# A recurrence's diagonal by elementwise products and a block of ones, and background TensorE work pinned behind the dense products

## The chip, the cores and the metric

One core of one Trainium2 chip runs the kernel. The metric is device time in microseconds (us) of one execution. Before the change the median of three runs is 1806.2 us (1805.67 to 1806.68). The profile is of one execution that took 1806.44 us; its span, from the first to the last instruction, is 1804.7 us, so 1.74 us lie around the span.

## The reference

One decoder layer on 256 positions of 2048 channels. A combined input projection feeds three branches (a gated delta rule with convolutions, the HGRN2 recurrence, attention into 256 memory tokens); gates mix them, and an MLP of width 8192 follows. What the change touches is the HGRN2 branch's matrix of scores within a chunk:

```python
def hgrn2(q, f, i, lb):
    ...
    def step(state, inp):
        q_i, k_i, v_i, b_i = inp
        dec = jnp.exp(jnp.where(causal[:, :, None], b_i[..., :, None, :] - b_i[..., None, :, :], -jnp.inf))
        a_i = jnp.einsum('bhtd,bhjd,bhtjd->bhtj', q_i, k_i, dec)
        o = (q_i * jnp.exp(b_i)) @ state + a_i @ v_i
```

On the diagonal (t = j) the decay is 1, so the diagonal of `a_i` is the sum over the 128 channels d of q times k.

## The kernel before

**Dense products.** Nearly all work is products of activations with weights streamed from memory. Weights come as blocks of 256 rows by 512 columns (one DMA of 512 KB by SyncE), are split by ScalarE (`wh`, L174) and VectorE (`wl = w - wh`, L175) into two fp32r parts, and TensorE sums three products: high by high, high by low, low by high. `unit` (L206 to L208) does it with 512 columns moving for each product, 12 products for a block; `unit_joined` puts the two parts of the activations side by side (L225, 512 columns) and adds the third product over 256 columns (L227). A `unit_joined` has 128 products in six pieces and writes two PSUM tiles, whose sums are taken out by ScalarE and VectorE (L265, L266) when their half is done; the pool has two such tiles, so the next unit's first half waits for the first tile to be read.

**Background steps.** The branches' own small work is written as Python generators in the list `bg`: `gen_start` (statistics, masks, transposes of x), `gen_ab`, `gen_c` (attention), `gen_a` (delta rule, once for each of two head groups), `gen_b` (HGRN2, once for each head group), `gen_merge`. After each piece of a dense unit `tick` adds the present rate to a credit, and `pump` runs as many steps (up to the next `yield`) of the first generator as the credit has whole numbers. A unit gives 8 ticks (a branch's own product 4), whatever its kind. The rates: 1.0 at the start, R1 while the delta rule's projections run, R2 in the memory branch's gates, R3 in the HGRN2 projections (`BF`, `BQ`, `BI`, `BZ` for each head group), R4 in branch 0's products. Steps from `ahead_of_all` (convolutions, gates) go in front of the list.

**Order.** The order in which the program is traced is a priority, not an order: the framework's scheduler, when it lays out each engine's queue, may put an instruction whose inputs it takes as ready ahead of older ones, and puts one that it takes as not ready behind younger ones. Each queue is then fixed, and an engine waits at its next instruction until that one's inputs are there. `pin` (`keep_in_program_order`) sets one instruction behind everything traced before it on its engine.

**The lines that matter below.** L495 (`gcol`), L498 (`pc`) and L507 (`pl`): three small transposes in three consecutive steps of `gen_start`. L637: four transposes of the softmax in `gen_c`. L793 to L800: the decay matrix of `gen_a`, in which VectorE writes `dl` (L796) and TensorE multiplies it (L798) within the same step. L1060 to L1067: the diagonal in `gen_b`; for each head and each half of the sequence a full 128x128 product of k and q in fp32 (L1064, 8 for a head group, which the trace shows as 16 records), of which VectorE keeps the diagonal by multiplying with the identity (L1066). L1127 to L1133: the predicated copies after the products `pa` (L1120).

Of the kernel before, what the change touches and what calls it, by code (L numbers as in the profile page):

```python
# [10 lines left out]
F32 = mybir.dt.float32  # L11
F32R = mybir.dt.float32r
I32 = mybir.dt.int32
AF = mybir.ActivationFunctionType
ALU = mybir.AluOpType
AX = mybir.AxisListType

P = 128
# [15 lines left out]
KG = 2  # L34
BL = 16
WB = 4
R1, R2, R3, R4 = 1.1, 1.0, 1.0, 1.2


@with_exitstack  # L40
def tile_trunk(ctx: ExitStack, tc, a):
    nc = tc.nc
    V, A, T, G = nc.vector, nc.scalar, nc.tensor, nc.gpsimd

    cst = ctx.enter_context(tc.tile_pool(name="cst", bufs=1))
    wp = ctx.enter_context(tc.tile_pool(name="wp", bufs=4))
# [15 lines left out]
    def g4(name, shape=(P, 1024), dt=F32):  # L62
        return gp.tile(list(shape), dt, tag="g", name=nm(name))
# [11 lines left out]
    def bank(name):  # L75
        return pbp.tile([P, 512], F32, tag="bp", name=nm(name))

    def const(name, shape, dt=F32):
        return cst.tile(list(shape), dt, tag=name, name=name)
# [8 lines left out]
    mem_r = a["mem"][0].rearrange("(t p) n -> p t n", p=P)  # L88
    x_r = a["x"][0].rearrange("(t p) n -> p t n", p=P)

    pin = tc.keep_in_program_order

    def adma(out, in_):
        tc.keep_in_program_order(nc.scalar.dma_start(out, in_))

# [32 lines left out]

    def pump(n=1):
        while n > 0 and bg:  # L130
            try:
                next(bg[0])
                n -= 1
            except StopIteration:
                bg.pop(0)

    def drain():
        while bg:
# [264 lines left out]


    mgt, mlt, caus = const("mgt", [P, P]), const("mlt", [P, P]), const("caus", [P, P])
    mgtr = const("mgtr", [P, P], F32R)
    msk2 = const("msk2", [P, 2, P])
    dblk = const("dblk", [P, BL])
    mblk = const("mblk", [P, P])
# [2 lines left out]
    def gen_masks():  # L412
        G.affine_select(out=mgt, in_=ones, pattern=[[-1, P]], base=0, channel_multiplier=1,
                        compare_op=ALU.is_gt, fill=0.0)
        G.affine_select(out=mlt, in_=ones, pattern=[[1, P]], base=0, channel_multiplier=-1,
                        compare_op=ALU.is_gt, fill=0.0)
        pin(V.tensor_tensor(out=caus, in0=mlt, in1=ident, op=ALU.add))
        pin(V.tensor_copy(mgtr, mgt))
        pin(V.tensor_copy(msk2[:, 0, :], mlt))
        pin(V.tensor_scalar(out=msk2[:, 1, :], in0=caus, scalar1=-1.0, scalar2=None, op0=ALU.mult))  # L420
        pin(V.tensor_reduce(out=dblk, in_=ident.rearrange("p (k c) -> p c k", c=BL), axis=AX.X, op=ALU.add))
        yield
        prev = ident
        for s in (1, 2, 4, 8, 16, 32, 64):
            b = 2 * s
            if b < P:
                cur = mblk if b == BL else cst.tile([P, P], F32, tag=f"blk{b.bit_length() % 2}", name=f"blk{b}")
                v3 = cur.rearrange("p (n s) -> p n s", s=b)
                G.affine_select(out=v3, in_=ones.rearrange("p (n s) -> p n s", s=b),
                                pattern=[[-b, P // b], [0, b]], base=0, channel_multiplier=1,  # L430
                                compare_op=ALU.is_ge, fill=0.0)
                G.affine_select(out=v3, in_=v3, pattern=[[b, P // b], [0, b]], base=b - 1,
                                channel_multiplier=-1, compare_op=ALU.is_ge, fill=0.0)
            else:
                cur = ones
            d = cst.tile([P, P], F32, tag="mdiff", name=f"mdiff{s}")
            pin(V.tensor_tensor(out=d, in0=cur, in1=prev, op=ALU.subtract))
            pin(V.tensor_tensor(out=mT[s], in0=d, in1=mlt, op=ALU.mult))
            prev = cur
            yield  # L440

    def bc(t, n):
        return t.unsqueeze(1).to_broadcast([P, n, P])
# [25 lines left out]
    def gen_start():  # L469
        V.tensor_copy(rsm, rstd_of(sumsq_of(ssm, "ssm"), NT, D))  # L470
        xs = []

        def load_x():
            c = len(xs)
            t = g4("x", (P, NT, 512))
            pin(nc.sync.dma_start(t, x_r[:, :, c * 512:(c + 1) * 512]))
            xs.append(t)

        masks = gen_masks()
        grow = load_grow(["g_pre_mix", "g_pre_mlp"], 16, adma)  # L480
        crow = const("crow", [96, P])
        adma(crow, a["conv_a"][0].rearrange("t (c p) -> (t c) p", p=P))
        lrow = const("lrow", [8, P])
        adma(lrow, a["lb_raw"][0].rearrange("(c p) -> c p", p=P))
        load_x()
        yield
        pb = bank("rb")
        for t in range(NT):
            rr = g4("rr", (P, P))
            V.tensor_scalar(out=rr, in0=ones, scalar1=rsm[:, t:t + 1], scalar2=None, op0=ALU.mult)  # L490
            T.matmul(pb[:, t * P:(t + 1) * P], rr, ident, start=True, stop=True)
        V.tensor_copy(rbm, pb[:, 0:S])
        yield
        load_x()
        turn_grow(grow, 32, 16)  # L495
        yield
        pc = bank("pc")
        T.transpose(pc[:, 0:96], crow, ident[0:96, 0:96])  # L498
        V.tensor_copy(ccol, pc[:, 0:96])
        for nm_, t in (("gn_a", gna), ("gn_b", gnb)):  # L500
            adma(t, a[nm_][0:1, :].to_broadcast([P, P]))
        adma(alog, a["a_log"][0:1, :].to_broadcast([P, 8]))
        adma(dtb, a["dt_bias"][0:1, :].to_broadcast([P, 8]))
        yield
        load_x()
        pl = bank("pl")
        T.transpose(pl[:, 0:8], lrow, ident[0:8, 0:8])  # L507
        raw, e, lb = small("raw", 8), small("e", 8), small("lb", 8)
        V.tensor_copy(raw, pl[:, 0:8])
        V.tensor_tensor(out=e, in0=raw, in1=raw, op=ALU.subtract)  # L510
        exp_ln_table(e, e)
        pin(A.activation(e, e, AF.Exp))
        re = small("re", 8)
        V.reciprocal(re, e)
        pr = small("pr", 8)
        V.tensor_tensor(out=pr, in0=e, in1=re, op=ALU.mult)
        V.tensor_tensor(out=lb, in0=pr, in1=pr, op=ALU.subtract)
        pin(A.activation(lbl1, lb, AF.Ln, bias=1.0, scale=-1.0))
        c1, c2 = small("c1", 8), small("c2", 8)
        V.tensor_scalar(out=c1, in0=lb, scalar1=TINY, scalar2=None, op0=ALU.max)  # L520
        pin(A.activation(c1, c1, AF.Ln))
        V.tensor_scalar(out=c2, in0=lb, scalar1=0.0, scalar2=-1e30, op0=ALU.is_le, op1=ALU.mult)
        V.tensor_tensor(out=lba, in0=c1, in1=c2, op=ALU.add)
        yield
        st = small("ssx", 8)
        sumsq_chunk(xs[0], st, 0)
        yield
        load_x()
        A.activation(alog, alog, AF.Exp)
        next(masks)  # L530
        yield
        sumsq_chunk(xs[1], st, 1)
        yield
        next(masks)
        yield
        sumsq_chunk(xs[2], st, 2)
        yield
        next(masks)
        yield
        sumsq_chunk(xs[3], st, 3)  # L540
        yield
        next(masks)
        yield
        rx = rstd_of(sumsq_of(st, "ssx"), NT, D)

        def scale(c):
            for t in range(NT):
                V.tensor_scalar(out=xs[c][:, t, :], in0=xs[c][:, t, :], scalar1=rx[:, t:t + 1],
                                scalar2=None, op0=ALU.mult)

        scale(0)
        yield
        for c in range(4):
            if c < 3:
                scale(c + 1)
            hc = h8("hh")
            hB[c], hT[c] = hc, (hc[:, :, 0, :], hc[:, :, 1, :])
            transpose_chunk(xs[c], hT[c], c, 16)
            yield
        yield from masks  # L560
# [209 lines left out]
    def gen_a(hg, kc, qc, vc, z):  # L770
# [20 lines left out]
        dec = g4("dec", (P, 8, P))  # L791
        for t in range(NT):
            dl = g4("dl", (P, 2, 4, P), F32R)  # L793
            pd = bank("dec")
            for i, l_ in enumerate((ldh, ldl)):
                V.tensor_tensor(out=dl[:, i], in0=bc(caus, 4),  # L796
                                in1=l_.bitcast(F32)[:, t, hs].unsqueeze(2).to_broadcast([P, 4, P]), op=ALU.mult)
                T.matmul(pd, mgtr, dl[:, i].rearrange("p h i -> p (h i)"), start=i == 0, stop=i == 1)  # L798
            A.activation(dec[:, t * 4:t * 4 + 4, :], pd.rearrange("p (h i) -> p h i", h=4), AF.Exp)
            yield  # L800
# [239 lines left out]
    def gen_b(hg, k, g, q, v, z):  # L1040
# [17 lines left out]
        yield  # L1058

        AT = g4("AT", (P, 8, P))  # L1060
        for t in range(NT):
            pd = bank("ad")
            for h in range(4):
                T.matmul(pd[:, h * P:(h + 1) * P], k[:, h, t * P:(t + 1) * P], q[:, h, t * P:(t + 1) * P],  # L1064
                         start=True, stop=True)
            V.tensor_tensor(out=AT.rearrange("p (h t) i -> p h t i", t=NT)[:, :, t, :],  # L1066
                            in0=pd.rearrange("p (h i) -> p h i", h=4), in1=bc(ident, 4), op=ALU.mult)  # L1067
        yield
        kps = [g4("kp0", (P, 4, S)), g4("kp1", (P, 4, S))]
        qp = lp.tile([P, 8, BL * BL], F32, tag="lb", name=nm("qp"))  # L1070
# [352 lines left out]
```

## Time and profile before

| | before |
|---|---|
| median of 3 runs | 1806.2 us |
| profiled execution | 1806.44 us |
| its span | 1804.7 us |
| TensorE products busy | 1793.5 us, 99% |
| TensorE weight loads busy | 1532.6 us, 85% |
| VectorE busy | 1127.0 us, 62% |
| ScalarE busy | 905.6 us, 50% |
| TensorE's share of the chain that ended last | 97% |
| granted TensorE clock | 1.0 in every stage but the tail |

A busy TensorE is not yet one without losses: the end of a product's record is modelled and reaches over the start of the next, so a short wait leaves no idle time in the table. What a product costs is read from start to start of neighbouring products.

### The profile page before, as it was taken

What the parts mean: (1) busy time and instruction counts of PE and PEld (TensorE: products, weight loads), DVE (VectorE), ACT (ScalarE), POOL (GpSimd) and SP (SyncE); (2) the same over time, 40 slices, a digit from 0 to 9 for tenths busy, and PEclk for the clock granted to TensorE, in tenths of its full rate; (3) what the DMA queues carried; (4) which work ended last, traced back from release to release, by engine and by line L of the source; (5) the groups of instructions that cost most, each with busy time, mean ns of one, the idle gap of its engine ahead of it and who ended that gap; (6) DMA issues with size and microseconds to landing.
All of it is one profiled execution on the core that took longest, in us unless ns stands there. A gap on an engine that the chain in (4) does not pass through costs nothing.

```text
span 1804.7 us, 23851 instructions
## 1 busy us (share of the span) xinstructions
PE 1793.5 (99%) x9241; PEld 1532.6 (85%) x9241; DVE 1127.0 (62%) x1518; ACT 905.6 (50%) x1156; POOL 44.5 (2%) x68
## 2 busy tenths in 40 slices
PE   9999999999999999999999999999999999999998
PEld 7888888888888888888888888888888888888886
DVE  5865678755764677696555557655655565655556
ACT  6645565544555565555444445544444444444433
POOL 1000000200200000000000000000000000000000
PEclk9999999999999999999999999999999999999999
DMA  8665645754665556465666674666666676666664
GB/s 264 207 194 160 185 146 168 209 172 138 177 187 152 158 169 187 141 186 175 198 186 187 213 232 152 191 193 191 195 186 198 188 220 187 195 187 195 188 194 139
DMA packets 174946, 333.40 MB, mean 185 GB/s; under 512 B 13144, under 2 KB 14832, under 8 KB 174576
## 3 DMA queue, kind: packets, MB, share of 16 engines
q1 hardware_dynamic: 169280, 325.10, 58.7%
q10 hardware_dynamic: 4528, 4.54, 0.9%
q0 software_dynamic: 1024, 2.23, 0.7%
q8 instruction: 72, 1.18, 0.3%
q14 instruction: 42, 0.34, 0.1%
HBM read 329.60 MB, written 2.23 MB: 184 GB/s over the span
## 4 chain that ended last, share of the span: by engine, by line
PE 97%; DVE 1%; DMA 1%; ACT 1%; issue 0%; SPq 0%; DVEq 0%; POOLq 0%; POOL 0%; ACTq 0%
PE mm L225 23%; PE mm L206 18%; PE mm L207 18%; PE mm L208 18%; PE mm L227 12%; PE pa L1120 1%; DMA w<-in_w_kv_mem 0%; PE pzt L921 0%; PE pw L916 0%; PE mm L373 0%; PE mm L375 0%; PE mm L372 0%; DVE wl L175 0%; DMA w<-in_w_in 0%; DVE cv L718 0%
## 5 line engine op out<-in xcount | busy, mean ns | idle before, releaser
L175 DVE TENSOR_TENSOR wl<-w,wh 128x1024 fp32r<-128x1024 f32 x600 | 728.5, 1223 | 540.2 <-ACT wh L174 456.3
L174 ACT CAST wh<-w 128x1024 fp32r<-128x1024 f32 x600 | 628.0, 1052 | 719.0 <-PE mm L208 453.7
L206 PE MATMUL mm<-wh,hh 128*128 128x512 f32 x576 | 227.5, 395 | 0.3 <-DVE sum L266 0.3
L208 PE MATMUL mm<-wh,hh 128*128 128x512 f32 x576 | 224.7, 390 | 0.0
L225 PE MATMUL mm<-h2h,wh 128*128 128x512 f32 x960 | 224.4, 390 | 0.0
L207 PE MATMUL mm<-wl,hh 128*128 128x512 f32 x576 | 224.4, 390 | 0.0
L225 PEld LDWEIGHTS mm<-h2h,wh 128*128 128x128 f32 x960 | 178.3, 188 | 35.8
L206 PE MATMUL mm<-wh,mh 128*128 128x512 f32 x512 | 199.2, 389 | 0.0
L207 PE MATMUL mm<-wl,mh 128*128 128x512 f32 x512 | 199.2, 389 | 0.0
L208 PE MATMUL mm<-wh,ml 128*128 128x512 f32 x512 | 199.2, 389 | 0.0
L225 PE MATMUL mm<-hh,wh 128*128 128x512 f32 x768 | 184.8, 391 | 0.3 <-ACT z L730 0.3
L225 PEld LDWEIGHTS mm<-hh,wh 128*128 128x128 f32 x768 | 141.0, 188 | 27.8 <-ACT z L730 0.5
L208 PEld LDWEIGHTS mm<-wh,hh 128*128 128x128 f32 x576 | 108.1, 188 | 22.7
L206 PEld LDWEIGHTS mm<-wh,hh 128*128 128x128 f32 x576 | 108.2, 188 | 21.8 <-DVE sum L266 0.5
L207 PEld LDWEIGHTS mm<-wl,hh 128*128 128x128 f32 x576 | 108.3, 188 | 21.1
L227 PEld LDWEIGHTS mm<-h2h,wl 128*128 128x128 f32 x960 | 119.3, 192 | 2.3
L227 PE MATMUL mm<-h2h,wl 128*128 128x256 f32 x960 | 120.3, 283 | 0.0
L207 PEld LDWEIGHTS mm<-wl,mh 128*128 128x128 f32 x512 | 96.1, 188 | 20.0
L208 PEld LDWEIGHTS mm<-wh,ml 128*128 128x128 f32 x512 | 96.1, 188 | 19.9
L206 PEld LDWEIGHTS mm<-wh,mh 128*128 128x128 f32 x512 | 96.1, 188 | 19.9
L227 PE MATMUL mm<-hh,wl 128*128 128x256 f32 x768 | 102.2, 284 | 0.0
L227 PEld LDWEIGHTS mm<-hh,wl 128*128 128x128 f32 x768 | 98.9, 191 | 3.4
(388 smaller groups left out, 1913.9 us busy)
## 6 DMA issues: line engine op xcount, KB each, us to landing
w<-in_w_in SPq DMA_DIRECT2D x240, 512.0 KB, 4.0
w<-in_w_mlp_in SPq DMA_DIRECT2D x128, 512.0 KB, 4.0
w<-in_w_mlp_out SPq DMA_DIRECT2D x128, 512.0 KB, 4.2
w<-in_w_out SPq DMA_DIRECT2D x32, 512.0 KB, 4.1
w<-in_w_kv_mem SPq DMA_DIRECT2D x30, 512.0 KB, 4.9
w<-in_w_br_c SPq DMA_DIRECT2D x16, 512.0 KB, 4.1
w<-in_w_br_a SPq DMA_DIRECT2D x16, 512.0 KB, 4.5
w<-in_w_br_b SPq DMA_DIRECT2D x16, 512.0 KB, 3.6
```

What stands on the lines that cost most here:

```text
L174: q(A.copy(wh[:, js, 0:width], w[:, js, 0:width]))
L175: q(V.tensor_tensor(out=wl[:, js, 0:width], in0=w[:, js, 0:width], in1=wh.bitcast(F32)[:, js, 0:width], op=ALU.subtract))
L206: T.matmul(o, st, wh[:, j, :], start=kt == 0, stop=False)
L207: T.matmul(o, st, wl[:, j, :], start=False, stop=False)
L208: T.matmul(o, sl, wh[:, j, :], start=False, stop=kt == nk - 1)
L225: T.matmul(ps[c], wh[:, j, c * P:(c + 1) * P], both[j], start=k0 + j == 0, stop=end)
L227: T.matmul(ps[c][:, 0:S], wl[:, j, c * P:(c + 1) * P], both[j][:, 0:S], start=False, stop=end)
L1120: T.matmul(pas[h][:, t * 192:t * 192 + 192], kp[:, h, t * P:(t + 1) * P], qp[:, h * 2 + t, 0:192], start=True, stop=True)
```

## The change

`gen_b` no longer forms full products for the diagonal. VectorE multiplies k and q elementwise for a whole head group (`kq`), ScalarE and VectorE split that into two fp32r parts (`kqh`, `kql`), and TensorE multiplies a 128x128 block of ones with each, 512 columns at a time; every row of the result then holds the sums over the channels, and VectorE keeps the diagonal as before. It takes three steps where it took one. `gen_a` makes `dl` in one step and multiplies it in the next, twice. `gen_start` has one more `yield`, ahead of the `pl` transpose. The first TensorE instruction of every background step is pinned. Rates R2 to R4 rise.

```diff
-R1, R2, R3, R4 = 1.1, 1.0, 1.0, 1.2
+R1, R2, R3, R4 = 1.1, 1.05, 1.05, 1.27
...
-    V, A, T, G = nc.vector, nc.scalar, nc.tensor, nc.gpsimd
+    V, A, G = nc.vector, nc.scalar, nc.gpsimd
+
+    pin = tc.keep_in_program_order
+    step_begins = [False]
+
+    class T:
+
+
+        @staticmethod
+        def placed(ins):
+            if step_begins[0]:
+                pin(ins)
+                step_begins[0] = False
+            return ins
+
+        @staticmethod
+        def matmul(*args, **kwargs):
+            return T.placed(nc.tensor.matmul(*args, **kwargs))
+
+        @staticmethod
+        def transpose(*args, **kwargs):
+            return T.placed(nc.tensor.transpose(*args, **kwargs))
...
     def pump(n=1):
         while n > 0 and bg:
+            step_begins[0] = True
             try:
                 next(bg[0])
                 n -= 1
             except StopIteration:
                 bg.pop(0)
+            step_begins[0] = False
...
-    mgtr = const("mgtr", [P, P], F32R)
+    mgtr, onesr = const("mgtr", [P, P], F32R), const("onesr", [P, P], F32R)
...
+        pin(V.tensor_copy(onesr, ones))
...
         load_x()
+        yield
         pl = bank("pl")
...
             dl = g4("dl", (P, 2, 4, P), F32R)
-            pd = bank("dec")
             for i, l_ in enumerate((ldh, ldl)):
                 V.tensor_tensor(out=dl[:, i], in0=bc(caus, 4),
                                 in1=l_.bitcast(F32)[:, t, hs].unsqueeze(2).to_broadcast([P, 4, P]), op=ALU.mult)
+            yield
+            pd = bank("dec")
+            for i in range(2):
                 T.matmul(pd, mgtr, dl[:, i].rearrange("p h i -> p (h i)"), start=i == 0, stop=i == 1)
...
         AT = g4("AT", (P, 8, P))
-        for t in range(NT):
-            pd = bank("ad")
-            for h in range(4):
-                T.matmul(pd[:, h * P:(h + 1) * P], k[:, h, t * P:(t + 1) * P], q[:, h, t * P:(t + 1) * P],
-                         start=True, stop=True)
-            V.tensor_tensor(out=AT.rearrange("p (h t) i -> p h t i", t=NT)[:, :, t, :],
-                            in0=pd.rearrange("p (h i) -> p h i", h=4), in1=bc(ident, 4), op=ALU.mult)
+        kq, kqh, kql = g4("kq"), g4("kqdh", dt=F32R), g4("kqdl", dt=F32R)
+        V.tensor_tensor(out=kq, in0=k.rearrange("p h s -> p (h s)"), in1=q.rearrange("p h s -> p (h s)"), op=ALU.mult)
+        yield
+        A.copy(kqh, kq)
+        V.tensor_tensor(out=kql, in0=kq, in1=kqh.bitcast(F32), op=ALU.subtract)
+        yield
+        for hp in range(2):
+            pd, cs = bank("ad"), slice(hp * 512, hp * 512 + 512)
+            T.matmul(pd, onesr, kqh[:, cs], start=True, stop=False)
+            T.matmul(pd, onesr, kql[:, cs], start=False, stop=True)
+            V.tensor_tensor(out=AT[:, hp * 4:hp * 4 + 4, :], in0=pd.rearrange("p (b i) -> p b i", b=4), in1=bc(ident, 4),
+                            op=ALU.mult)
         yield
```

## Rows read from the trace of the kernel before

**Rows 1.** The page: busy us (share) and instructions; the chain's shares by engine.
```profile
PE 1793.5 (99%) x9241; PEld 1532.6 (85%) x9241; DVE 1127.0 (62%) x1518; ACT 905.6 (50%) x1156; POOL 44.5 (2%) x68
...
PE 97%; DVE 1%; DMA 1%; ACT 1%; issue 0%; SPq 0%; DVEq 0%; POOLq 0%; POOL 0%; ACTq 0%
```

**Rows 2.** Costliest groups: operation xcount | busy us, mean ns | idle before, releaser.
```profile
L175 DVE TENSOR_TENSOR wl<-w,wh 128x1024 fp32r<-128x1024 f32 x600 | 728.5, 1223 | 540.2 <-ACT wh L174 456.3
L174 ACT CAST wh<-w 128x1024 fp32r<-128x1024 f32 x600 | 628.0, 1052 | 719.0 <-PE mm L208 453.7
```

**Rows 3.** The chain in order of time: start us, us, what.
```profile
633.35 1.79 PE ad L1064 x16
769.65 1.78 PE ad L1064 x16
1133.24 7.28 PE mm L225 x32
```

**Rows 4.** Timeline, TensorE at both `dec`: start us, us, operation xcount [idle <-releaser].
```profile
275.27 0.63 PE L225 MATMUL mm<-hh,wh 128*128 128x512 f32 x2
...
276.41 0.19 PEld L798 LDWEIGHTS dec<-dl,mgtr 128*128 128x128 f32 x1 [0.24 <-DVE dl L796]
...
276.75 2.93 PE L225 MATMUL mm<-hh,wh 128*128 128x512 f32 x12
...
460.06 0.39 PE L208 MATMUL mm<-wh,ocl 128*128 128x512 f32 x1
...
461.29 0.40 PE L207 MATMUL mm<-wl,och 128*128 128x512 f32 x1
```

**Rows 5.** Timeline, TensorE around the transposes of `gen_start`.
```profile
36.33 0.48 PE L206 MATMUL mm<-wh,memT 128*128 128x512 f32 x1
...
36.74 0.24 PE L106 MATMUL gcol<-ident,grow 32*128 32x32 f32 x1
...
37.14 0.22 PE L507 MATMUL pl<-ident,lrow 8*128 8x8 f32 x1
...
37.63 0.40 PE L208 MATMUL mm<-wh,memT 128*128 128x512 f32 x1
```

**Rows 6.** Timeline, TensorE around two small transposes of another step.
```profile
159.40 0.88 PE L227 MATMUL mm<-hh,wl 128*128 128x256 f32 x6
160.21 0.30 PE L673 MATMUL abt<-ident,abT 32*128 32x32 f32 x2
160.44 0.96 PE L225 MATMUL mm<-hh,wh 128*128 128x512 f32 x3
```

**Rows 7.** Timeline, TensorE at the start of the second head group's `AK`.
```profile
257.07 0.60 PE L637 MATMUL pT<-ident,p 128*128 128x128 f32 x4
...
257.43 0.72 PE L227 MATMUL mm<-hh,wl 128*128 128x256 f32 x4
...
258.46 2.12 PE L225 MATMUL mm<-hh,wh 128*128 128x512 f32 x8 [0.32 <-ACT z L730]
```

**Rows 8.** Timeline where `BQ` of head group 1 gives way to `BI`.
```profile
664.48 1.11 PE L227 MATMUL mm<-hh,wl 128*128 128x256 f32 x8
...
665.13 0.67 DVE L266 TENSOR_TENSOR sum<-mm,sum 128x512 f32<-128x512 f32 x1
...
665.86 0.50 PE L206 MATMUL mm<-wh,hh 128*128 128x512 f32 x1 [0.26 <-DVE sum L266]
```

**Rows 9.** Timeline, VectorE and TensorE ahead of the second diagonal.
```profile
762.34 1.21 DVE L175 TENSOR_TENSOR wl<-w,wh 128x1024 fp32r<-128x1024 f32 x1
...
764.28 0.39 PE L207 MATMUL mm<-wl,hh 128*128 128x512 f32 x1
...
768.01 1.22 DVE L1056 TENSOR_TENSOR bm<-bm,bd 128x1024 f32<-128x1024 f32 x1
```

**Rows 10.** Who waited for whom, 190 to 660 us: us in total, times, longest.
```profile
PEld oc L604 <- ACT pT L281: 0.5, 2, 0.3
```

More of the change, by code (lines that the diff above doesn't have):

```diff
@@ L89, in tile_trunk @@
     x_r = a["x"][0].rearrange("(t p) n -> p t n", p=P)
-    pin = tc.keep_in_program_order
     def adma(out, in_):
```

## The prediction

> **What bounds the kernel now.** I read the shares and the chain first, then the chain in order of time, then the timeline wherever TensorE's products stand further apart than usual. TensorE is busy for 99% of the span and makes up 97% of the chain [rows 1]; VectorE's and ScalarE's largest groups are the weight splits, and before them both engines idle for hundreds of microseconds, ScalarE mostly until TensorE gives a weight buffer back [rows 2]. So the splits are ahead and TensorE sets the end. Its price for a product is read from start to start: 32 products over 512 columns take 7.28 us, 0.2275 each [rows 3]. The reader is to see that a TensorE instruction saved is time saved nearly one to one, that work on the other engines is free as long as the splits stay ahead, and that the waits left on TensorE are few and below a microsecond each [rows 4, 7, 8, 10].
>
> **The change part by part.** The sum is made against the profiled execution, 1806.44 us, which lies 0.24 above the median of the runs; the 0.24 comes off at the end.
>
> *The diagonal.* Removed: for each of two head groups 8 fp32 products, 16 records, 1.79 and 1.78 us of the chain [rows 3]. Added: for each group 4 fp32r products over 512 columns, whose form the dense ones have, 4 x 0.2275 = 0.91. Both lie on TensorE's path: 3.57 - 1.82 = 1.75 us saved. If the ones cost as much as the two `dec` products with their waits do, (1.48 - 3 x 0.2275) / 2 = 0.40 each (the 1.48 is worked out below) [rows 4], only 0.38 is left; I take 1.75, since with their inputs made a step earlier they stand as the dense products do. The Trainium skill (TensorE: Matmul & The Clock Gate, Back-to-back issue gap) gives about 131 ns as the sustained spacing of products over 512 columns; by that the new ones would cost 0.52 a group, the saving would be 2.53 and the time 0.78 lower. This trace has 0.2275, so the trace decides.
>
> Off the path the diagonal adds an elementwise product (1.22 us for this shape on VectorE [rows 9]), a cast (1.05 on ScalarE) and a subtraction (1.22 on VectorE) [rows 2], 3.49 us a group and 7.0 in all; the two multiplications with the identity stay. The cover is the lead of the splits. It is thinnest just ahead of the second diagonal: a split that ends at 763.55 is used at 764.28, 0.73 later [rows 9]. The new VectorE work comes behind it. It costs nothing while the lead there is over 1.22, and at most 2.44 - 0.73 = 1.7 if both VectorE operations come ahead of one split with such a lead. I take 0, because ScalarE and VectorE idle before most splits [rows 2]. The copy that makes the block of ones is a single operation in the early masks and costs nothing.
>
> *The decay matrix.* `dl` and its product are in one step now, and TensorE waits for VectorE [rows 4]. From 275.27 to 276.75 start five products (two dense, `dec`, dense, `dec`), 1.48 us instead of 5 x 0.2275 = 1.14; from 460.06 to 461.29 four, 1.23 instead of 0.91. The split into two steps puts a step's worth of dense products between, so I take back 0.34 + 0.32 = 0.66; the bounds are 0 and 0.66. Two steps more for each delta-rule group only shift what follows.
>
> *The pins.* I counted ticks and steps through the program and compared each background step's place with TensorE's order in the trace. Only four first instructions stand ahead of their place, so only there does a pin move anything. Three are `gcol`, `pc` and `pl`: they stand within 0.6 us, between an L206 and the L207 of the same triple [rows 5], where the program has 12 products between each two. Together with two dense products they take 37.63 - 36.33 = 1.30 us, so 0.85 without those. Apart, each visit pays for its own way in and out: two small transposes of another step begin 0.09 late (six products of 0.12 from 159.40 end at 160.12), take 0.23, and the dense ones behind them lose 0.11 (0.96 - 0.39 = 0.57 for two spacings) [rows 6]. With one transpose each that is some 0.36, three times 1.08: 0.23 lost. Bounds 0 and 3 x 0.43 - 0.85 = 0.44. The queues that these steps are moved past lose nothing that I see: SyncE's third load of x stays in its step, the fourth and what follows come one step, some 2.7 us, later, and the transposes of x they feed run two dense units before their first use.
>
> The fourth is the softmax's transposes (L637), which my count puts 12 products later. Now they fill 0.36 us (257.07 to 257.43) of a time in which TensorE must wait anyway for ScalarE to empty PSUM (`z`, which releases it at 258.46) [rows 7]. Behind the pin TensorE reaches that wait 0.36 earlier and does the transposes later: 0.36 lost. Bounds 0 (ScalarE comes to `z` earlier) and 0.44. Behind a pinned instruction younger dense products may still be put ahead of it, so no queue is blocked by a pin alone.
>
> *Shifted steps.* Where a joined unit ends, the next one waits for VectorE to empty a PSUM tile. At 664.48 eight products of 0.12 should end at 665.44, and the next starts at 665.86, 0.42 late, because the predicated copies of L1127 to L1133 were ahead of L266 on VectorE [rows 8]. With two more steps and R3 at 1.05 my count puts the `pa` products before those copies exactly at the end of that unit, so the copies fall behind L266, and this wait goes. But some seven such boundaries get other background work beside them, and one of seven was hit before. I take 0, with 0.42 either way. The step budget closes as before: by the count, the last TensorE step of HGRN2 falls behind the last product of branch 0 with either set of rates, so no steps pile up at the drain.
>
> Sum: -1.75 - 0.66 + 0.23 + 0.36 = -1.82; 1806.44 - 1.82 - 0.24 = 1804.4 us.
>
> **The rivals.** In all, 0.2% (3.6 us) is about what a measurement of this kernel can tell from no change.
>
> (a) The pins don't move what I say (the four are held back by something else, or the scheduler fills the places alike): without the 0.59 it is 1803.8. For: only four of some hundred steps are concerned.
>
> (b) A wash: the `dec` waits return one step later, one more boundary is hit (0.42), and one split comes late by 1: 1806.2 - 1.75 + 0.59 + 0.42 + 1 = 1806.5. For: leads as short as 0.73 [rows 9].
>
> (c) VectorE becomes the bound where HGRN2 runs. The place is the second head group's start, the price at most all of the new work, 7.0, less what TensorE saves (1.75 + 0.66): 1806.2 + 7.0 - 2.4 = 1810.8, slower by 0.25%. It decides from the point where the new work eats the lead of several splits in a row; against it speak the idle times before the splits [rows 2].
>
> (d) Everything aligns: the waits for `pT` (0.5 [rows 10]), for `z` (257.43 plus four products is 257.99, the next starts at 258.46: 0.47 [rows 7]) and the boundary's 0.42 go as well, and the pins cost nothing: 1806.2 - 1.75 - 0.66 - 0.5 - 0.47 - 0.42 = 1802.4, faster by 0.21%. Against: by my count the steps of the attention (`gen_c`), where the first two of these waits lie, keep their places, R1 being unchanged.
>
> (e) TensorE is not the bound: weight loads are busy for 85% [rows 1], and if the rest is room, the saved products fall into it and the time stays at 1806.2. The Trainium skill (Perfetto Trace Analysis, Identifying the Most-Contended Engine) says to judge TensorE by weight loads, not by product time. The chain and the even spacing of 0.2275 speak against that here [rows 1, 3].
>
> **How the numbers follow.** Forecast 1804.4: 0.62. (a) 1803.8: 0.10. (b) 1806.5: 0.12. (c) 1810.8: 0.06. (d) 1802.4: 0.07. (e) 1806.2: 0.03. The forecast's own bounds are 1806.2 - 1.75 - 0.66 - 0.42 = 1803.4 and, with `dec` giving nothing, the pins at 0.88 and a boundary at 0.42, 1805.8. To leave out no more than 2 in 10 the range takes in (a), (e) and the most of (b): 1802.9 to 1806.5. Faster by over 0.2%: 0.07, (d). Slower: 0.06, (c). Within: 0.87.
>
> **What would show it.** In the changed kernel's trace: the `ad` products 0.91 us a group and spaced as dense ones; `dec` without VectorE as releaser; `gcol`, `pc`, `pl` a dozen dense products apart; the L637 transposes of the fourth head behind the wait for `z`, and that wait near 0.8; no wait for `sum` at the end of the second `BQ`. It is wrong if TensorE shows idle time released by a weight split around the second diagonal, or if the time leaves the span's TensorE work by more than the waits listed.

## The result and the profile after

| | before | after |
|---|---|---|
| median of 5 runs | 1806.02 us (1805.67 to 1806.68) | 1813.54 us (1812.92 to 1815.8) |
| profiled execution | 1806.44 us | 1812.92 us |
| its span | 1804.7 us | 1811.2 us |

The ratio is 1.0044, with a 95% interval of [1.0034, 1.0055]: the change made the kernel 7.5 us slower. The forecast was 1804.4 us, its range ended at 1806.5, and of the rivals only (c) had a slower end, with 1810.8 and another place.

In the listing after, every TensorE product has L60 and every transpose L64 (the wrapper's lines); a weight split is `wl` L196 and `wh` L195, a joined unit's sum L286 and L287, the forward substitution L903 to L914.

The page's list of the costliest groups, in the columns of [rows 2], has one new entry: idle time ahead of TensorE's dense products that VectorE's `sum` ended.

```profile
PE 1794.2 (99%) x9217; PEld 1530.7 (85%) x9217; DVE 1130.5 (62%) x1523; ACT 907.6 (50%) x1158; POOL 40.1 (2%) x68
...
L60 PE MATMUL mm<-hh,wh 128*128 128x512 f32 x768 | 185.8, 393 | 5.5 <-DVE sum L287 4.7
```

The busy shares are those of [rows 1]; they hide the loss. The view of who waited for whom, TensorE alone over the whole span (us in total, times, longest), names it:

```profile
PE mm L60 <- DVE sum L287: 4.7, 1, 4.7
...
PE mm L60 <- ACT z L753: 0.8, 1, 0.8
...
PE mm L60 <- DVE wl L196: 0.2, 1, 0.2
```

One wait of 4.7 us stands out of a list in which nothing from the kernel's middle had reached 1. The timeline of TensorE there, where `BF` of the first head group gives way to `BQ`:

```profile
528.58 3.82 PE L60 MATMUL mm<-hh,wh 128*128 128x512 f32 x16
532.23 1.11 PE L60 MATMUL mm<-hh,wl 128*128 128x256 f32 x8
538.08 3.41 PE L60 MATMUL mm<-hh,wh 128*128 128x512 f32 x8 [4.74 <-DVE sum L287]
541.29 1.38 PE L60 MATMUL mm<-hh,wl 128*128 128x256 f32 x8
542.50 2.00 PE L60 MATMUL mm<-hh,wh 128*128 128x512 f32 x8
```

The eight products over 256 columns from 532.23 take some 0.95 (eight equal ones in e5 below, from 535.20 to 536.15), so TensorE was ready at 533.18 and began at 538.08, 4.90 late. And then it is slow: the first eight take 541.29 - 538.08 = 3.21 where 8 x 0.2275 = 1.82 [rows 3] would do. The table by windows (us, TensorE's busy time and instructions, granted clock, DMA share, GB/s) shows why:

```profile
533.00:538.00 5.00, 0.34 (x3) 1.00 0.42 131
538.00:541.50 3.50, 3.42 (x9) 0.57 0.49 151
541.50:545.00 3.50, 3.50 (x22) 0.94 0.00 0
```

After the idle time the granted clock is 0.57 for 3.5 us, near the lower of its two levels (1.2 of 2.4 GHz), then 0.94. The two lots of eight products after the wait lose 1.39 and 0.25. The place costs 4.90 + 1.64 = 6.5 of the 6.5 us by which the two spans differ.

VectorE at that place (start us, us, operation):

```profile
521.55 1.23 DVE L196 TENSOR_TENSOR wl<-w,wh 128x1024 fp32r<-128x1024 f32 x1 [2.91 <-ACT wh L195]
522.85 0.17 DVE L903 MEMSET lb<- 128x128 f32 x1
...
536.12 1.22 DVE L914 TENSOR_TENSOR X<-xc,mblk 128x1024 f32<-128x1024 f32 x1
537.26 1.28 DVE L287 TENSOR_TENSOR sum<-mm,sum 128x512 f32<-128x512 f32 x2
```

and in the kernel before:

```profile
517.48 0.17 DVE L878 MEMSET lb<- 128x128 f32 x1
...
529.72 1.23 DVE L889 TENSOR_TENSOR X<-xc,mblk 128x1024 f32<-128x1024 f32 x1
530.87 0.68 DVE L266 TENSOR_TENSOR sum<-mm,sum 128x512 f32<-128x512 f32 x1
```

with the TensorE products that this `sum` lets begin:

```profile
532.82 1.98 PE L225 MATMUL mm<-hh,wh 128*128 128x512 f32 x8
```

Between `lb` and `X` lies the second delta-rule group's forward substitution: fifteen pairs of small operations (a product and a reduction, 0.17 to 0.29 each), every one of which needs the one before, with some weight splits among them. In both kernels the whole block, 13.4 us before and 14.4 after from `lb` to the start of `sum`, stands ahead of `sum` in VectorE's queue. Before, `sum` ended at 531.55 and TensorE needed it at 532.82: 1.27 to spare. Now the chain begins behind one split more, 5.4 us later (522.85 - 517.48), and is 1.0 longer, for it has five splits inside where it had four. Less the 1.27 and the 0.36 by which TensorE itself comes later (533.18 against 532.82), that is 4.8 of the 4.9. ScalarE's part of the sum is there long before VectorE comes to it:

```profile
533.43 1.06 ACT L286 COPY sum<-mm 128x512 f32<-128x512 f32 x2
```

From 534.49 on, only `X` and what stands ahead of it hold `sum`. (ScalarE is late as well: two splits went ahead of L286. With VectorE free at 534.0, when the first half is there, `sum` would end at 534.7 and TensorE would still have waited 1.5.)

The other places, by the difference in start of the same dense product in the two traces (counted from the first): 0.62 is lost between products 96 and 192, 0.66 more by product 2360, 6.87 from there to product 2688 (the place above, and 0.3 besides), 1.38 is won back by product 3136, 0.37 by 3712, and 0.17 lost to the end.

The remaining rows of after that answer to those of before. The small transposes of `gen_start`, to be held against [rows 5]:

```profile
36.28 0.48 PE L60 MATMUL mm<-wh,memT 128*128 128x512 f32 x1
36.88 0.50 PE L60 MATMUL mm<-wl,memT 128*128 128x512 f32 x1
37.22 0.63 PE L60 MATMUL mm<-wh,memT 128*128 128x512 f32 x2
...
39.61 0.24 PE L64 MATMUL gcol<-ident,grow 32*128 32x32 f32 x1
...
42.67 0.25 PE L64 MATMUL pc<-ident,crow 96*128 96x96 f32 x1
...
48.34 0.22 PE L64 MATMUL pl<-ident,lrow 8*128 8x8 f32 x1
```

The softmax's transposes [rows 7], the second group's decay matrix [rows 4] and the second diagonal [rows 3], with the late split ahead of it [rows 9]:

```profile
259.13 2.12 PE L60 MATMUL mm<-hh,wh 128*128 128x512 f32 x8 [0.75 <-ACT z L753]
...
261.57 0.60 PE L64 MATMUL pT<-ident,p 128*128 128x128 f32 x4
...
463.95 0.39 PE L60 MATMUL mm<-wh,ocl 128*128 128x512 f32 x1
464.32 0.47 PE L60 MATMUL dec<-dl,mgtr 128*128 128x512 f32 x1
464.63 0.40 PE L60 MATMUL mm<-wh,och 128*128 128x512 f32 x1
464.86 0.48 PE L60 MATMUL dec<-dl,mgtr 128*128 128x512 f32 x1
465.18 0.40 PE L60 MATMUL mm<-wl,och 128*128 128x512 f32 x1
...
771.35 0.50 PE L60 MATMUL mm<-wl,hh 128*128 128x512 f32 x1 [0.19 <-DVE wl L196]
...
779.42 0.40 PE L60 MATMUL ad<-kqdh,onesr 128*128 128x512 f32 x1
...
780.36 0.39 PE L60 MATMUL mm<-wh,hh 128*128 128x512 f32 x1
```

The four new products of the diagonal take 780.36 - 779.42 = 0.94.

### The profile page after: what moved, and what is told of

Read it like the earlier page. It is cut to its first block, busy times and chain, and to the rows that moved or that the text cites. A ratio compares the mean times of both kernels' runs of the same rounds, so it can differ in the third digit from the quotient of the medians.

```text
span 1811.2 us, 23809 instructions
## 1 busy us (share of the span) xinstructions
PE 1794.2 (99%) x9217; PEld 1530.7 (85%) x9217; DVE 1130.5 (62%) x1523; ACT 907.6 (50%) x1158; POOL 40.1 (2%) x68
## 4 chain that ended last, share of the span: by engine, by line
PE 83%; DVE 2%; ACT 1%; issue 1%; POOL 0%; DVEq 0%; POOLq 0%
PE mm L60 78%; PE pa L60 1%; PE pzt L60 1%; PE pw L60 1%; DVE wl L196 0%; PE kk L60 0%; PE o L60 0%; PE bo L60 0%; PE tr L64 0%; PE y L60 0%; PE mgT L64 0%; PE X L64 0%; DVE xc L911 0%; DVE tm L910 0%; ACT wh L195 0%
## 5 line engine op out<-in xcount | busy, mean ns | idle before, releaser
L196 DVE TENSOR_TENSOR wl<-w,wh 128x1024 fp32r<-128x1024 f32 x600 | 729.0, 1223 | 540.8 <-ACT wh L195 460.8
L195 ACT CAST wh<-w 128x1024 fp32r<-128x1024 f32 x600 | 628.4, 1052 | 723.1 <-PE mm L60 642.6
L60 PE MATMUL mm<-wh,hh 128*128 128x512 f32 x1152 | 366.4, 392 | 0.0
L60 PEld LDWEIGHTS mm<-wh,hh 128*128 128x128 f32 x1152 | 216.1, 188 | 44.0
L60 PE MATMUL mm<-wl,hh 128*128 128x512 f32 x576 | 224.7, 390 | 0.2 <-DVE wl L196 0.2
L60 PE MATMUL mm<-h2h,wh 128*128 128x512 f32 x960 | 224.4, 390 | 0.0
L60 PEld LDWEIGHTS mm<-h2h,wh 128*128 128x128 f32 x960 | 178.3, 188 | 35.8
L60 PE MATMUL mm<-wh,mh 128*128 128x512 f32 x512 | 199.2, 389 | 0.0
L60 PE MATMUL mm<-wl,mh 128*128 128x512 f32 x512 | 199.2, 389 | 0.0
L60 PE MATMUL mm<-wh,ml 128*128 128x512 f32 x512 | 199.2, 389 | 0.0
L60 PE MATMUL mm<-hh,wh 128*128 128x512 f32 x768 | 185.8, 393 | 5.5 <-DVE sum L287 4.7
L60 PEld LDWEIGHTS mm<-hh,wh 128*128 128x128 f32 x768 | 141.9, 189 | 33.5 <-issue 4.9
L60 PEld LDWEIGHTS mm<-wl,hh 128*128 128x128 f32 x576 | 108.3, 188 | 22.3 <-DVE wl L196 1.1
L60 PEld LDWEIGHTS mm<-h2h,wl 128*128 128x128 f32 x960 | 119.1, 192 | 2.3
L60 PE MATMUL mm<-h2h,wl 128*128 128x256 f32 x960 | 120.2, 283 | 0.0
L60 PEld LDWEIGHTS mm<-wh,mh 128*128 128x128 f32 x512 | 96.1, 188 | 20.0
L60 PEld LDWEIGHTS mm<-wl,mh 128*128 128x128 f32 x512 | 96.1, 188 | 20.0
L60 PEld LDWEIGHTS mm<-wh,ml 128*128 128x128 f32 x512 | 96.1, 188 | 19.8
L60 PEld LDWEIGHTS mm<-hh,wl 128*128 128x128 f32 x768 | 99.1, 192 | 3.6
L60 PE MATMUL mm<-hh,wl 128*128 128x256 f32 x768 | 101.8, 284 | 0.0
L60 PE MATMUL mm<-wh,oh 128*128 128x512 f32 x128 | 50.3, 393 | 0.0
L60 PE MATMUL mm<-wh,mgh 128*128 128x512 f32 x128 | 50.0, 390 | 0.0
```

Of the source, the lines that this page charges most:

```text
L60: return T.placed(nc.tensor.matmul(*args, **kwargs))
L195: q(A.copy(wh[:, js, 0:width], w[:, js, 0:width]))
L196: q(V.tensor_tensor(out=wl[:, js, 0:width], in0=w[:, js, 0:width], in1=wh.bitcast(F32)[:, js, 0:width], op=ALU.subtract))
```

## The experiments

Theory A: the loss is one place in a fixed queue. The steps added to the delta rule (the decay matrix in two steps) and R2 = 1.05 lay the second group's substitution so that VectorE does all of it, one split later than before, ahead of the sum that TensorE needs. Rival B: the chain simply comes too late, and the later the worse. Rival C: pins, or the new VectorE work of the diagonal, cost it wherever the chain is. Each run is held against the kernel before on the same chip (medians 1806.18 for the first four runs, 1805.55 for the next four, 1806.00 for the last four).

**One part undone, one part alone.** `e1_dec_one_step` is the changed kernel with the decay matrix in one step again:

```diff
             for i, l_ in enumerate((ldh, ldl)):
...
-            yield
             pd = bank("dec")
```

> The changed kernel with the one yield taken out that parts dl from its product (gen_a has its old number of steps, two fewer for a head group; rates, pins and diagonal stay). Theory: 6.2 of the lost microseconds are one place, where the boundary BF0 to BQ0 waits 4.7 us on VectorE for sum (L287) behind the serial forward substitution (L910, L911) of the second delta-rule group, and TensorE then runs seven products at half clock. That chain sits there because the two extra steps moved it. Then this kernel has no wait over 1 us there and takes 1813.5 - 6.2 + 0.6 (the waits at dec come back) = 1807.9 us, within 1 us. Rival, the higher rates moved it, or the pins: the wait stays and it takes 1813 or more.

Measured: 1806.91, ratio 1.0004 [0.9994, 1.0014]. The wait for `sum` is gone. The chain begins at 513.78 and `X` ends at 527.24, far ahead of the sum, though TensorE now waits 0.6 for `X` itself.

`e2_no_pins` is the changed kernel without pins:

```diff
         def placed(ins):
-            if step_begins[0]:
-                pin(ins)
-                step_begins[0] = False
             return ins
```

> The changed kernel with no background instruction pinned; all else stays. Theory: pins move four instructions only, and VectorE's queue around the boundary is the same: the wait of 4.7 us stays, and only the 0.44 at the softmax's transposes (the wait for z, 0.9 instead of 0.47) and some 0.3 in gen_start come back: 1812.8 us. Rival, the pins cause the loss: 1806 to 1808 and no wait over 1 us at the boundary.

Measured: 1810.96, ratio 1.0026 [1.0016, 1.0037]; 2.7 better than the change against the kernel before (0.7 was expected), but most of the loss stays. TensorE now waits in another place for the same chain: unpinned, the transposes of `X` stand ahead of the dense products in its queue.

```profile
PE XT L61 <- DVE X L911: 4.1, 1, 4.1
```

So pins aren't the cause (rival C, first half). Of the 2.7, 0.7 is the shorter wait (4.06 by the timeline, against 4.74), and 1.0 to 1.3 is the pins' own price (e9, below); the rest isn't accounted for.

`e3_dec_split_alone` is the kernel before with the decay matrix in two steps:

```diff
-            pd = bank("dec")
             for i, l_ in enumerate((ldh, ldl)):
...
+            yield
+            pd = bank("dec")
+            for i in range(2):
...
```

> The kernel before with the decay matrix in two steps alone (old rates, no pins, old diagonal). Theory: the loss depends on where the chain stands against sum in VectorE's queue. Here, with the old rate R2, it stands so much later that sum comes inside it, ahead of its long part: no wait over 1.5 us, 1806.0 - 0.3 = 1805.7, between 1805 and 1807.5. Rival, any delay of the chain by two steps costs the boundary: 4 to 8 us more than before, 1810 to 1814.

Measured: 1805.69, ratio 0.9997 [0.9988, 1.0007]. With R2 at 1.0 the same two steps do no harm: the chain begins at 526.84, even later than in the changed kernel, but `sum` stands inside it, at 529.18. That already speaks against rival B.

`e4_diagonal_alone` is the kernel before with the new diagonal and the old rates:

```diff
+        kq, kqh, kql = g4("kq"), g4("kqdh", dt=F32R), g4("kqdl", dt=F32R)
...
+            T.matmul(pd, onesr, kqh[:, cs], start=True, stop=False)
+            T.matmul(pd, onesr, kql[:, cs], start=False, stop=True)
```

> The kernel before with the new diagonal alone (three steps, ones block; old rates, no pins, decay matrix as it was). Theory: the diagonal is a gain of its own, 0.77 us for a head group as the changed kernel shows: 1806.0 - 1.5 = 1804.5 us, within 0.7. Rival, the new VectorE and ScalarE work costs more than TensorE saves: 1807 or more, with waits for weight splits around the second diagonal.

Measured: 1806.03, ratio 0.9999 [0.9989, 1.0008]: a miss. By product 3136 it is 1.40 ahead of the kernel before, as in the changed kernel, but at the end of branch 0 there is a new wait:

```profile
PE oT L766 <- DVE on L757: 1.7, 1, 1.7
```

The diagonal has two steps more in each group; with the old R3 and R4 the last steps come up against the end of the branch and their transposes are waited for. The prediction said that the budget closes "with either set of rates"; it doesn't, and raising R3 and R4 is a part of the diagonal's price.

**Moving the chain.** `e5_chain_one_step_later` is the changed kernel with one empty step for the second group ahead of the substitution, the run on which A and B differ most:

```diff
+        for _ in range(1 * hg):
+            yield
         NB = P // BL
```

> The changed kernel with one empty step added ahead of the second delta-rule group's forward substitution, so that this chain comes about 12 dense products (2.7 us) later still. Theory A (the loss is one place in VectorE's fixed queue: the whole chain stands ahead of the sum that TensorE needs at the boundary from BF to BQ): with the added step the framework lays the sum into the middle of the chain, so the wait of 4.9 us and the slow products behind it (about 1.3) go: 1813.5 - 6.2 = 1807.3, within 0.8, and no wait for `sum` above 1 us there. Rival B (the chain simply comes too late, and the later the worse): the wait grows by up to 2.7 us, 1813.5 to 1816.3. Rival C (pins or the new VectorE work cost it, wherever the chain is): 1813.5.

Measured: 1807.37, ratio 1.0011 [1.0002, 1.002]. Later by a step, and 5.7 better against the kernel before of its batch (+1.8 in place of +7.5). Rival B falls. VectorE and then TensorE at the place:

```profile
525.81 0.17 DVE L905 MEMSET lb<- 128x128 f32 x1
...
534.57 0.27 DVE L912 TENSOR_TENSOR tm<-xc,lb 128x104 f32<-128x104 f32 x1
534.75 0.69 DVE L287 TENSOR_TENSOR sum<-mm,sum 128x512 f32<-128x512 f32 x1
535.36 0.25 DVE L913 TENSOR_REDUCE xc<-tm 128x8 f32<-128x104 f32 x1
...
540.03 1.23 DVE L916 TENSOR_TENSOR X<-xc,mblk 128x1024 f32<-128x1024 f32 x1
```

```profile
535.20 1.12 PE L60 MATMUL mm<-hh,wl 128*128 128x256 f32 x8
536.15 2.00 PE L60 MATMUL mm<-hh,wh 128*128 128x512 f32 x8
```

The chain begins 3.0 later than in the changed kernel and ends 3.9 later, and TensorE doesn't wait, for the framework has laid `sum` between the two halves of a pair. (The profiled execution is 1.7 above the median; it has a weight that landed late near 349, and a granted clock of 0.50 from 351.4 to 354.7 behind the two waits of 0.8 that this caused.)

`e12_chain_one_step_earlier` moves the chain the other way, by joining the two steps of `d2`:

```diff
                             in1=msk2.unsqueeze(1).to_broadcast([P, 4, 2, P]), op=ALU.mult)
-            yield
+        yield
```

> The changed kernel with one step less in each delta-rule group ahead of the substitution: the two multiplications `d2` are in one step, so all that follows in the group comes 12 dense products (2.7 us) earlier. Theory A: the chain starts ahead of the weight split that it now stands behind, ends near 531, and the sum is there before TensorE needs it at 533: no wait for `sum` above 1, 1807.3 within 0.8. Together with the run that moves the chain one step the other way, it would show that the place between the two is the bad one. Rival C (pins or VectorE's new work): 1813.5.

Measured: 1806.70, ratio 1.0004 [0.9995, 1.0013]. Each head group has a step less, so the second group's chain comes two steps earlier, not one: it begins at 517.67, 5.2 ahead of the changed kernel's and about where it was before the change. `X` ends at 531.1, and no wait for `sum` is left; TensorE waits 0.7 for `X`. Rival B would expect that as well; together with e5 it says that two steps earlier or one step later the 6 us are gone, and that the changed kernel stands in the bad place between.

`e6_rate2_back` is the changed kernel with one number changed:

```diff
-R1, R2, R3, R4 = 1.1, 1.05, 1.05, 1.27
+R1, R2, R3, R4 = 1.1, 1.0, 1.05, 1.27
```

> The changed kernel with R2 put back from 1.05 to 1.0 and nothing else; pins, decay matrix in two steps and the new diagonal stay. Theory A (the chain's place against the sum, set by the decay matrix's added steps and R2 together): the sum again stands inside the chain, the wait at the boundary from BF to BQ goes, 1807.3 within 0.8; the late decay product at 464 may come back into step, which would give 1807.0. Rival C (pins, decay steps or the diagonal's VectorE work cost it, not the rates): 1813.5.

Measured: 1805.79, ratio 1.0002 [0.9992, 1.0011]; 7.3 better than the change, and 0.4 below the lowest that A expected (1807.0 less its 0.8). Part of that is seen in the starts of the dense products: between products 192 and 2240 it loses nothing where the change loses 0.66, and between 3136 and 3712 it gains 0.81 where the change gains 0.37, for the late split at 771 is not there. Its pins, decay steps and diagonal are those of the change. Its chain begins at 528.13, 5.3 later than in the change, and `sum` stands inside it, at 530.46: once more later, and better. So neither the decay split (e3) nor R2 (which e1 has) costs the time; the two together do. And rival C falls. What is left of TensorE's waits beside the start:

```profile
PE mm L60 <- ACT z L753: 0.7, 1, 0.7
```

**The wait as a dose.** `e10_chain_three_columns_less` and `e11_chain_one_column_less` shorten the chain of the changed kernel (3 in the first, 1 in the second; both leave out that part of the result):

```diff
         for c in range(BL - 2, -1, -1):
+            if hg == 1 and c < 3:
+                if c % 2 == 0:
+                    yield
+                continue
```

> The changed kernel, in which the second delta-rule group's substitution leaves out its last three columns (six operations of 0.27 to 0.29 on VectorE; that part of the result is left out). Their steps stay. One split more stands ahead of the sum than was behind the chain before. Theory (the wait is the length of what stands ahead of the sum): the sum would end at about 535.2 instead of 537.9, so TensorE's wait falls from 4.9 to about 2.0 to 2.2 us: 1810.6 if the products behind it still run at half clock, 1809.3 if they don't. Rival (the wait comes from something else that is late, such as the weight or the sum's first half on ScalarE): the wait stays near 4.9 and the time at 1813.5.

> As the run before, with the last column alone left out (two operations of 0.29; that part of the result is left out). The smaller dose of the same cut: by the order of VectorE's queue the sum ends at about 536.4, the wait falls from 4.9 to about 3.3, and the time to 1811.9 if the half clock behind it stays, 1810.6 without. Rival: 1813.5.

Measured: 1810.68, ratio 1.0025 [1.0014, 1.0036], and 1811.69, ratio 1.0031 [1.0021, 1.0041]. The waits, of e10 and then of e11:

```profile
PE mm L60 <- DVE sum L287: 2.0, 1, 2.0
```

```profile
PE mm L60 <- DVE sum L287: 3.2, 1, 3.2
```

Both are as worked out from the order of the queue, 2.0 to 2.2 and 3.3: down to 2.0 at least, the wait is as long as what stands ahead of `sum` on VectorE. The two windows (the wait, then the products behind it) of e10 and of e11 differ in the clock:

```profile
535.30:537.20 1.90, 0.00 (x0) 1.00 0.12 47
537.20:540.40 3.20, 3.17 (x9) 0.58 0.77 184
```

```profile
533.00:536.20 3.20, 0.01 (x1) 1.00 0.04 15
536.20:538.20 2.00, 1.97 (x9) 1.00 0.77 193
```

After 2.0 us without work the clock was 0.58, after 3.2 it was 1.00. So the slow products don't follow from the wait's length alone; what decides stays open. (e11's profiled execution, in which the clock held, took 1809.5, 2.2 less than its median.)

**The pins' own price.** `e9_pins_alone` is the kernel before with the wrapper around TensorE's instructions and the step ahead of `pl`:

```diff
+        def placed(ins):
+            if step_begins[0]:
+                pin(ins)
...
         load_x()
+        yield
         pl = bank("pl")
```

> The kernel before with the pins and the added step ahead of `pl`, nothing else. Theory: what the pinned kernels' traces show on TensorE, 0.62 for `gcol`, `pc` and `pl` apart and about 0.4 at the wait for `z`, is all that pins cost: 1805.8 + 1.0 = 1806.8, range 1806.4 to 1807.3, and no wait for `sum` above 1. Rival: by the medians of the two kernels that differ in the pins (and R2 alike), 2.4: 1808.2. Rival: pins are the cause of the long wait at the boundary: 1812.

Measured: 1807.31, ratio 1.0007 [0.9998, 1.0017]: +1.3, at the upper end of the expected range, with an interval that takes in no change. By the same dense products it loses 0.59 at `gen_start`, between products 96 and 192, and 0.43 at the wait for `z`. Another 0.27 is lost in the attention, at product 1056, but that isn't the pins': the split ahead of it began later because its weight came later (219.10 against 218.82 before), and the pinned kernels e6 and e11 gain 0.16 at the same product. So the traces give the pins 1.0, and the 0.3 above it is open.

**What is worth keeping.** `e7_diagonal_with_rates` is the kernel before with the new diagonal of e4 and R3, R4 as in the change; `e8_diagonal_rates_dec` has the decay split of e3 too:

```diff
-R1, R2, R3, R4 = 1.1, 1.0, 1.0, 1.2
+R1, R2, R3, R4 = 1.1, 1.0, 1.05, 1.27
```

> The kernel before with the new diagonal and R3, R4 raised as in the change; no pins, decay matrix in one step, R2 at 1.0. Theory: the diagonal saves about 0.77 a group, 1.53; with the raised rates the steps end before branch 0 does, so the wait of 1.7 for the transposes of the last output, which the diagonal alone with the old rates had at 866.89, is gone; the wait of 0.42 from the second BQ to BI goes too: 1806.2 - 1.53 - 0.42 = 1804.2, range 1803.6 to 1804.8. Rival (the diagonal is worth nothing whatever the rates, since its VectorE work delays splits): 1806.0.

> As the run before (new diagonal, R3 and R4 raised, R2 at 1.0, no pins), with the decay matrix in two steps as well: all of the change but the pins and R2. Theory: the sum stands inside the substitution's chain as it did with the decay split alone, so there is no long wait, and the split adds the 0.5 that it gave alone: 1804.2 - 0.5 = 1803.7, range 1803.0 to 1804.5; with the run that puts back R2 alone, the difference is the cost of the pins, 2 to 3.5. Rival (two steps more in each delta-rule group bring the long wait whatever R2 is): 1810.

Measured: 1804.68, ratio 0.9994 [0.9985, 1.0004], and 1803.43, ratio 0.9989 [0.998, 0.9999]. The wait at the end of branch 0 is gone in both. e7 lies in its expected range by the bare time, but against the kernel before of its batch it won 0.9 where 2.0 was expected: the same chain takes back a part, now through the transposes of `X`, which the raised R3 brings closer to it, and between products 2240 and 2688 it loses 1.06:

```profile
529.84 1.09 PE L897 MATMUL XT<-ident,X 128*128 128x128 f32 x8 [0.75 <-DVE X L890]
```

With the decay split the chain has `sum` inside again, and 2.1 is won of the 2.5 expected. e8 is faster than both kernels: 2.1 us below the kernel before and, by the differences to it, 9.6 below the changed one. It is the change without the pins, the step ahead of `pl` and the raise of R2. (e6 differs from it in the pins and that step alone, and by 2.4 in the medians where e9 has 1.3. The profiled executions of the two are 1.2 apart; e6's runs reach from 1804.58, the profiled one, to 1808.34, and what makes the others longer isn't shown.)

## Why the prediction was wrong

**The step that failed: "Shifted steps".** The prediction let the added steps "only shift what follows" and put what the shift does at the boundaries between dense units at "0, with 0.42 either way"; the raise of R2 has no term in it. At one boundary the two together cost 6.5. The prediction saw the right kind of event: it described how a joined unit's next one waits for VectorE to empty a PSUM tile, with predicated copies ahead of L266 as the reason [rows 8]. It took the price of the one case in the trace, 0.42, as the price of any. But what a boundary costs is the length of what VectorE's queue has ahead of the sum, and a block as long as the substitution's 13.4 us isn't in the prediction. The trace had it: before the change the chain ended right ahead of a sum, and that sum had 1.27 to spare. The prediction counts the steps' places in the program, which spreads the substitution over eight steps; VectorE's queue has it back to back, but for the splits. The 5.4 is a net shift: the four steps more ahead of the chain, two in each group, push it later (by 9.4 in e3), and R2's rise brings it back (528.13 in e6, 522.85 in the change). Had it been known, the 5.4 less the 1.27 would have given 4.1 of wait; 4.9 was measured. But a larger shift isn't a longer wait: in e3, e5 and e6 the chain is later still and `sum` passes through it.

That the queue keeps its order is seen in e5 against the change: `sum` waits its turn behind `X` in one and passes through the chain in the other, though ScalarE's part is there in both. The Trainium skill (PSUM — Partial Sum Buffer, Engine vs sequencer instructions) says that VectorE's queue is strictly first in, first out; these two traces agree: in the change `sum` begins at 537.26, as `X` ends, though the first half of ScalarE's part is there at 534.0.

**The half clock behind the wait** wasn't in the prediction at all: 1.6 of the 6.5.

**Pins: right mechanism, too small.** Predicted 0.59; by the starts of the same products 0.62 at `gen_start` and 0.43 at the wait for `z`, 1.05 in all (0.59 and 0.43 in e9, with +1.3 by its median). The three visits apart cost no more than the 1.08 predicted: from the dense product ahead of each to the second behind it are 0.84, 0.58 and 0.81, where two spacings are 0.455; that is 0.38, 0.13 and 0.35 each, 0.86 together. (The prediction's 0.36 for a visit is a little high by its own rows: 0.43 less half of the 0.23 is 0.32.) But taking them out of the old place saves far less than the 0.85 of the prediction: the 1.30 of [rows 5], from 36.33 to 37.63, is still 0.94 without them (the same three starts, 36.28 to 37.22 in the rows above), for the step ahead of them, `rb`, pays its way out there anyway. Only 0.36 was theirs, so 0.86 - 0.36 = 0.50 goes by these rows, and 0.59 to 0.62 by product 192, where the prediction's bound was 0.44. The wait for `z` is as predicted in kind and size: the fourth head's transposes stand behind it, it is 0.8, and 0.43 is lost (0.36 predicted).

**The decay matrix: half right.** The first group's products follow each other without a wait (the pair at 279.13 takes 0.48). The second group's gained nothing: from 463.95 to 465.18 there are four starts in 1.23, exactly the 1.23 of [rows 4], for `dl` and its products fall together there all the same. That is R2's rise again: in e6, with R2 at 1.0, the same pair starts at 468.00 and 468.24 without a gap. In the sum 0.66 was taken; e3, where only this is changed, won 0.5 by its median.

**The diagonal: right.** Predicted 0.91 a group, measured 0.94; 1.78 - 0.94 = 0.84 saved for each. No trace shows TensorE waiting behind the VectorE work that I costed at nothing. The prediction's own sign of being wrong did appear, a split that comes late around the second diagonal, where the prediction had put its thin lead of 0.73 [rows 9]: TensorE starts the product of 771.35 late by 0.35. But the new work stands behind that split in VectorE's queue, and what stands ahead of it is old work:

```profile
769.30 0.91 DVE L1082 MEMSET bR<- 128x1024 f32 x1 [0.16 <-issue]
770.13 1.16 DVE L196 TENSOR_TENSOR wl<-w,wh 128x1024 fp32r<-128x1024 f32 x1
771.21 1.21 DVE L1087 TENSOR_TENSOR kq<-ft,sum 128x1024 f32<-128x1024 f32 x1
```

It takes R2 for that: e6, e7 and e8 have the same diagonal, R3 and R4, but R2 at 1.0, and no late split there. So this too is a shifted step. Rival (c) was wrong in its cause; the time that it gave, 1810.8, is near the one measured by luck.

**The boundary from `BQ` to `BI`** is gone as counted, and with it the 0.42 (0.55 by the starts of the dense products). e4, which has the old R3, is 1.40 ahead by product 3136 as well, so the diagonal's two steps are enough for it; R3 isn't needed, as the prediction had it. **The step budget** doesn't close by itself (e4).

**The other rivals.** Of the three waits that (d) let go, the boundary's went, `z` grew and `pT` stayed in part. Against (e), e4 gains what the diagonal saves on TensorE nearly one to one, until branch 0 ends. (a) and (b) were both out of reach of the loss.

**Put together,** without the one place the two spans would be level (6.5 - 6.5), where the sum had -1.8: pins cost 0.5 more, the decay matrix gave 0.3 less, and the late split took 0.5 (0.35 and 0.11 at the next product); against the 0.55 that the boundary gave stand some 1.1 in small places, among them 0.3 between products 2360 and 2688, 0.2 after product 3712 and 0.1 at product 1056, which I didn't follow one by one.

## What to carry to other kernels

Before steps are added or a rate is raised, look in the trace of before for long blocks of dependent small operations in an in-order queue, and for each evacuation behind one, how much it has to spare; a shift beyond that is paid in full, and a shift a little further may cost nothing. Where such a knife edge shows, try the neighbours (a step or two earlier, one later) before a change is given up: here the diagonal, its rates and the decay split were worth 2.1 us together, and R2 and the pins hid it.

## What the runs showed of the hardware that was not expected

The granted clock fell to the lower of its two levels for some 3 us behind an idle time in the middle of dense work: 0.57 after 4.9 us idle in the changed kernel, 0.50 after 4.1 us in e2, 0.58 after 2.0 us in e10 (the stretches read differ a little), and 0.50 in e5 after two waits of only 0.8 us. But it stayed at 1.00 after 3.2 us in e11, and in e10 near 351 behind two waits like those of e5 (0.5 and 0.8). Where it fell behind a wait of 2.0 to 4.9 us, the slow products cost 1.5 to 1.7 us over the wait's own length; when it falls, these runs don't tell.
